# The probabilities of two attentions are scaled by 1/sum on ScalarE instead of VectorE

## The chip, the core and the metric

The kernel runs on one core of a Trainium2 chip. The metric is the device time of one launch in microseconds (us). Before the change three runs took 2502.02 to 2503.47 us, with a median of 2502.81.

The engines are named as the profile names them: PE is TensorE's matmuls, PEld its weight loads, DVE is VectorE, ACT is ScalarE, POOL is GpSimd, SP is SyncE. Each works through its own queue of instructions in order and waits on semaphores for the others.

## The reference

The program is a hybrid layer (convolution beside an attention over the 256 best keys, or fewer, then a mixture of 64 experts) followed by two more layers: one with latent attention (MLA) and a SwiGLU, one with differential attention and a SwiGLU. 512 tokens, 1024 channels, 8 heads in each attention, all in f32. The change touches the softmax of the first two attentions. In the first layer (`dsa_attention`) it is

```python
s = jnp.einsum('bqhd,bqkhd->bhqk', qb, ks).astype(jnp.float32) * (Dh ** -0.5)
s = jnp.where(valid[:, None], s, -jnp.inf)
p = jax.nn.softmax(s, axis=-1).astype(vs.dtype)
o = jnp.einsum('bhqk,bqkhd->bqhd', p, vs)
```

and in the latent attention (`_mla_mixer`)

```python
logits = jnp.where(_chunk_mask(i * Q_BLOCK, s), logits * scale, NEG_BIG)
p = jax.nn.softmax(logits, axis=-1)
o = jnp.einsum('bhqk,bkhd->bqhd', p.astype(v.dtype), v, preferred_element_type=jnp.float32)
```

## The kernel before, in words

Every f32 product that must keep its precision is made from three matmuls (`mm3`, L228 to L230) of operands split into a high and a low part. `split` (L220, L221) makes these: ACT copies the high part, then DVE subtracts it from the source to get the low part. Names ending in h and l, such as `pth` and `ptl`, `qth` and `qtl`, `wh` and `wl`, are such pairs.

The first layer's and the latent attention share `attend`. Its items are the pairs (head h, query tile qt), 8 heads by 4 tiles of 128 queries, 32 in each attention. Tile qt sees `nk` = (qt + 1) * 128 keys, so four tiles of a head are 128, 256, 384 and 512 columns wide. Each item goes through five stages, and `pipeline` runs, in step s, stage A of item s, B of item s - 1, C of item s - 2, F of item s - 4 and E of item s - 3, in this order:

- A: logits, matmuls into a PSUM bank (L228 to L230, and L818 or L1859 for the mask).
- B: `soft_exp`. DVE takes the row maximum, negated (`nm`, L923), ACT the exponential with `nm` as its bias and the row sum as a second output (`p` and `sum`, L926; the read of the accumulator is an instruction of its own).
- C: DVE takes `rsum`, the reciprocal of `sum` (L943), and multiplies `p` by it in place (L945).
- E: `place` transposes `p` by matmuls with the identity, a 128x128 block each (L233), and splits the result: ACT `pth` (L220), DVE `ptl` (L221).
- F: for the last tile of a head alone, the value product from `pth` and `ptl`, and the split of its result (`qth`/`qtl` in the first layer, `mixoh`/`mixol` in the latent attention).

After the stages of a step `pipeline` takes units from a generator of other work ("filler" below), on average 1.2 a step in the first layer (the rest of the convolution, then half of the output projection, L792 to L799, L847, L848) and 0.8 in the latent attention (the projections of the next pairs of heads, `qd`, `kd`, `vd`, then half of the output projection, L1687). The filler fetches weights, each with a wide split on ACT and DVE (`wh`, `wl`, 128x1536 to 128x2048). Everything is issued in the order in which the Python code runs, so the order on each engine is that of the steps. The tiles `p` rotate through three buffers, `sum` through six. The differential attention has a softmax of its own, with a multiply at another line (L2047), and does not use `attend`.

Of the kernel before, what the change touches and what calls it, by code (L numbers as in the profile page):

```python
# [15 lines left out]
AF = mybir.ActivationFunctionType  # L16
OP = mybir.AluOpType
# [163 lines left out]
class _K:  # L181
# [747 lines left out]
    def attend(self, heads, logits, value, fill=None, n=0, bufs=3, ready=None):  # L929

        V = self.nc.vector
        lg, pr, pT = {}, {}, {}

        def A(h, qt):
            lg[h, qt] = logits(h, qt)

        def B(h, qt):
            pr[h, qt] = self.soft_exp(lg.pop((h, qt)), (qt + 1) * 128, "p", bufs)

        def C(h, qt):  # L940
            p, sm = pr[h, qt]
            rs = self.sm([128, 1], "rsum", bufs=4)
            V.reciprocal(rs, sm)  # L943
            nk = (qt + 1) * 128
            V.tensor_scalar(p[:, :nk], p[:, :nk], rs, None, OP.mult)  # L945

        def E(h, qt):
            if qt == 0:
                pT[h] = [self.slot(F32R, x).rearrange("p (a b) -> p a b", b=512) for x in ("pth", "ptl")]
            self.place(pT[h], qt, pr.pop((h, qt))[0])  # L950

        def F(h, qt):
            if qt == NT - 1:
                value(h, pT.pop(h))
        self.pipeline([(h, qt) for h in heads for qt in range(NT)], [(A, 0), (B, 1), (C, 2), (F, 4), (E, 3)], fill, n, ready)
# [1200 lines left out]
```

## Time and profile before

| | us |
|---|---|
| median of three runs | 2502.81 |
| the profiled execution | 2503.96 |
| its span, first to last instruction | 2502.2 |
| PE busy | 2321.1 (93%) |
| DVE busy | 1449.6 (58%) |
| ACT busy | 941.1 (38%) |
| L945, 64 instructions on DVE | 24.8 |

The profiled execution is one launch under the hardware profiler, and all rows are of it. Busy time is summed over the span and says nothing on the place. The chain of waits is followed back from the last instruction: at each piece either the instruction before it on its engine, or the one that released it. A row of the view of waits tells how long an engine sat idle in front of a line and what ended that; where the profile could not tell a semaphore's releaser it says "issue". A row of a timeline gives start, duration, engine, line, operation and tiles, and in brackets the idle time before it. PEclk is the granted clock of TensorE as a share of its higher level, 2.4 GHz; 0.50 is the lower one, 1.2 GHz. L945 runs from 265.0 to 1399.4 us, in two stretches of 32 instructions.

### The profile page before, as it was taken

How to read it: one execution, taken by the hardware profiler on the slowest of the kernel's cores; microseconds unless marked ns; L12 is line 12 of the kernel's file. 1: busy time of each engine (PE TensorE's matmuls, PEld its weight loads, DVE VectorE, ACT ScalarE, POOL GpSimd, SP SyncE). 2: the span in 40 equal slices, each digit the busy share in tenths (PEclk: the TensorE clock that was granted, in tenths of full speed). 3: DMA queues.
4: the chain of work that ended last, by engine and by line, in shares of the span. 5: the costliest groups of instructions: out<-in, count | busy, mean ns of one | idle time of the engine just before them, and what ended most of it. 6: DMA issues, size and time to landing. Idle time of an engine off the chain costs nothing.

```text
span 2502.2 us, 29499 instructions
## 1 busy us (share of the span) xinstructions
PE 2321.1 (93%) x11088; PEld 1805.0 (72%) x11088; DVE 1449.6 (58%) x2454; ACT 941.1 (38%) x1382; POOL 281.6 (11%) x184
## 2 busy tenths in 40 slices
PE   8877998799989999999699999999999998999998
PEld 4655767567667776676577788888888876888886
DVE  4599666666666765665576653333655657433235
ACT  1552443345545555555244222222234432322121
POOL 0652000122322222231000000000000000000000
PEclk9888999899999999999899999999999998999999
DMA  9442134599998999999402332232231121323310
GB/s 335 169 143 68 51 114 169 175 318 339 331 321 284 378 352 335 369 375 332 125 18 83 103 118 73 96 118 76 83 119 51 51 102 55 114 84 116 102 69 34
DMA packets 195009, 422.15 MB, mean 169 GB/s; under 512 B 21329, under 2 KB 99921, under 8 KB 186545
## 3 DMA queue, kind: packets, MB, share of 16 engines
q1 hardware_dynamic: 169984, 353.44, 39.8%
q0 software_dynamic: 12944, 39.20, 6.7%
q10 hardware_dynamic: 11938, 27.62, 3.0%
q8 instruction: 88, 1.44, 0.2%
q14 instruction: 55, 0.45, 0.1%
HBM read 390.78 MB, written 35.52 MB: 170 GB/s over the span
## 4 chain that ended last, share of the span: by engine, by line
PE 68%; DVE 16%; DMA 9%; ACT 4%; issue 2%; POOL 1%; ACTq 0%; SPq 0%; DVEq 0%; POOLq 0%
PE b L228 20%; PE b L229 19%; PE b L230 19%; PE b L1412 6%; DMA wraw<-in_w_dram 5%; DVE wl L221 4%; PE b L233 4%; DMA acc<-eo,isc 3%; ACT wh L220 2%; DVE work L754 1%; PE b L547 1%; DVE m L750 1%; DMA wraw<-in_w_ada_dram 1%; PE b L2029 1%; DVE y L1651 1%
## 5 line engine op out<-in xcount | busy, mean ns | idle before, releaser
L221 DVE TENSOR_TENSOR wl<-wraw,wh 128x2048 fp32r<-128x2048 f32 (+2 forms) x247 | 557.4, 2260 | 515.5 <-ACT wh L220 465.4
L220 ACT ACTIVATE wh<-wraw 128x2048 fp32r<-128x2048 f32 (+2 forms) x247 | 463.3, 1880 | 152.6 <-DVE wl L221 64.6
L228 PE MATMUL b<-xtl,wh 128*128 128x512 f32 (+1 forms) x928 | 343.5, 370 | 2.9 <-DVE xtl L221 2.9
L229 PE MATMUL b<-xth,wl 128*128 128x512 f32 (+1 forms) x928 | 341.6, 368 | 0.0
L230 PE MATMUL b<-xth,wh 128*128 128x512 f32 (+1 forms) x928 | 341.5, 368 | 0.0
L228 PE MATMUL b<-wl,xet 128*128 128x512 f32 x536 | 231.4, 432 | 15.3 <-DVE wl L221 14.9
L1412 PE MATMUL b<-wraw,aet 128*128 128x512 f32 x536 | 242.0, 595 | 0.8 <-ACT aet L1404 0.8
L230 PE MATMUL b<-wh,xet 128*128 128x512 f32 x536 | 214.2, 400 | 0.0
L229 PE MATMUL b<-wh,xet 128*128 128x512 f32 x536 | 213.1, 398 | 1.1 <-DVE xet L221 0.9
L228 PEld LDWEIGHTS b<-xtl,wh 128*128 128x128 f32 x928 | 176.1, 190 | 32.7 <-DVE xtl L221 3.6
L230 PEld LDWEIGHTS b<-xth,wh 128*128 128x128 f32 x928 | 175.8, 189 | 28.7
L229 PEld LDWEIGHTS b<-xth,wl 128*128 128x128 f32 x928 | 176.0, 190 | 28.0
L1412 PEld LDWEIGHTS b<-wraw,aet 128*128 128x128 f32 x536 | 98.9, 191 | 101.6 <-issue 97.0
L1217 POOL DMA_INDIRECT acc<-eo,isc x67 | 111.4, 1662 | 517.4 <-DMA acc<-eo,isc 126.9
L228 PE MATMUL b<-wl,ath 128*128 128x512 f32 x352 | 137.1, 390 | 0.0
L230 PE MATMUL b<-wh,ath 128*128 128x512 f32 x352 | 136.9, 389 | 0.0
L229 PE MATMUL b<-wh,atl 128*128 128x512 f32 x352 | 136.9, 389 | 0.0
L228 PEld LDWEIGHTS b<-wl,xet 128*128 128x128 f32 x536 | 103.2, 193 | 42.5 <-issue 20.3
L926 ACT ACTIVATE p<-b,nm 128x128 f32<-128x128 f32 (+3 forms) x128 | 67.0, 526 | 166.8 <-DVE nm L923 128.0
L229 PEld LDWEIGHTS b<-wh,xet 128*128 128x128 f32 x536 | 102.8, 192 | 28.6 <-issue 6.5
L230 PEld LDWEIGHTS b<-wh,xet 128*128 128x128 f32 x536 | 102.6, 191 | 23.1
L1933 ACT ACTIVATE t2k<-b 128x512 f32<-128x512 f32 x44 | 26.3, 599 | 185.9 <-PE b L230 185.9
(456 smaller groups left out, 4115.8 us busy)
## 6 DMA issues: line engine op xcount, KB each, us to landing
wraw<-in_w_dram SPq DMA_DIRECT2D x256, 512.0 KB, 11.2
wraw<-in_w_dram SPq DMA_DIRECT2D x64, 1024.0 KB, 9.7
wraw<-in_ffn_w_gu_dram SPq DMA_DIRECT2D x44, 1024.0 KB, 5.1
wraw<-in_w_ada_dram SPq DMA_DIRECT2D x24, 1024.0 KB, 10.4
wraw<-in_ffn_w_down_dram SPq DMA_DIRECT2D x20, 1024.0 KB, 4.9
wraw<-in_diff_w_in_dram SPq DMA_DIRECT2D x12, 1024.0 KB, 5.2
wraw<-in_w_in_dram SPq DMA_DIRECT2D x8, 1024.0 KB, 8.0
wraw<-in_w_in_dram SPq DMA_DIRECT2D x12, 512.0 KB, 5.0
```

The lines of the kernel that those rows point to most:

```text
L220: nc.scalar.activation(H, x, AF.Copy)
L221: nc.vector.tensor_tensor(out=L, in0=x, in1=H.bitcast(F32), op=OP.subtract)
L228: mm(ps, s[0], m[1], start=start, stop=False)
L229: mm(ps, s[1], m[0], start=False, stop=False)
L230: mm(ps, s[0], m[0], start=False, stop=stop)
L233: self.nc.tensor.transpose(ps, x, self.ident[:x.shape[0], :x.shape[0]])
L547: nc.tensor.matmul(ps, cb[:, kc, :], w[:, kk, :], start=False, stop=kc == 7)
L750: V.max(m8[qt - 1], work(qt))
L926: nc.scalar.activation(p[:, :nk], ps[:, :nk], AF.Exp, bias=nm, accum_out=sm)
L1217: nc.gpsimd.indirect_dma_start(out=acc, out_offset=IndirectOffsetOnAxis(ap=idx, axis=0), in_=o, in_offset=None, compute_op=OP.add)
L1412: nc.tensor.matmul(ps, aT[:, f * 128:f * 128 + 128], w[:, f, c], start=f == 0, stop=f == 1)
L1933: nc.scalar.activation(sg, pss[j], AF.Silu)
```

## The change

One line of `attend`'s stage C:

```diff
             rs = self.sm([128, 1], "rsum", bufs=4)
             V.reciprocal(rs, sm)
             nk = (qt + 1) * 128
-            V.tensor_scalar(p[:, :nk], p[:, :nk], rs, None, OP.mult)
+            self.nc.scalar.activation(p[:, :nk], p[:, :nk], AF.Copy, scale=rs)
```

The reciprocal stays on DVE. The multiply becomes an activation of the function Copy with a per-row scale, in place. PE, POOL and SP keep their instructions and their order; the matmuls that transpose `p` wait for ACT where they waited for DVE.

On ACT, in the first layer (the steps around 355 to 362 us; `p` are the probabilities, `rsum` the reciprocal of their sum, `pth` the high part of the transposed ones). Before:

```order
L926 ACTIVATE p,sum<-b,nm 128x512 [waits DVE_49]
L220 ACTIVATE pth<-b 128x2x128 [waits PE_49]
L926 ACTIVATE p,sum<-b,nm 128x128 [waits DVE_49]
L220 ACTIVATE pth<-b 128x3x128 [waits PE_49]
L926 ACTIVATE p,sum<-b,nm 128x256 [waits DVE_49]
L220 ACTIVATE pth<-b 128x4x128 [waits PE_49]
```

and now:

```order
L926 ACTIVATE p,sum<-b,nm 128x512 [waits DVE_49,Activation_49]
L945 ACTIVATE p<-p,rsum 128x384 [waits DVE_49,Activation_49]
L220 ACTIVATE pth<-b 128x2x128 [waits PE_49]
L926 ACTIVATE p,sum<-b,nm 128x128 [waits DVE_49,Activation_49]
L945 ACTIVATE p<-p,rsum 128x512 [waits DVE_49,Activation_49]
L220 ACTIVATE pth<-b 128x3x128 [waits PE_49]
L926 ACTIVATE p,sum<-b,nm 128x256 [waits DVE_49,Activation_49]
L945 ACTIVATE p<-p,rsum 128x128 [waits DVE_49,Activation_49]
L220 ACTIVATE pth<-b 128x4x128 [waits PE_49]
```

Between the exponential of one item and the copy `pth` of the item two before it now stands the scale of the item between them.

On DVE, in the latent attention, behind a weight split (around 1339 to 1346 us; `wl` is the low part of the weights, `qd` and `kd` are the next heads' queries and keys). Before:

```order
L221 TENSOR_TENSOR wl<-wraw,wh 128x2048
L224 SCALAR_TENSOR_TENSOR qd<-b,qd 128x512
L923 TENSOR_REDUCE nm<-b 128x1
L943 RECIPROCAL rsum<-sum 128x1
L945 TENSOR_SCALAR p<-p,rsum 128x384
L221 TENSOR_TENSOR ptl<-b,pth 128x2x128
L221 TENSOR_TENSOR kd<-b,kd 128x512
```

and now:

```order
L221 TENSOR_TENSOR wl<-wraw,wh 128x2048
L224 SCALAR_TENSOR_TENSOR qd<-b,qd 128x512
L923 TENSOR_REDUCE nm<-b 128x1
L943 RECIPROCAL rsum<-sum 128x1
L221 TENSOR_TENSOR ptl<-b,pth 128x2x128
L221 TENSOR_TENSOR kd<-b,kd 128x512
```

Here `ptl` follows `rsum` at once, and the transposes of the 384-wide `p` no longer wait for DVE.

## Rows read from the trace of the kernel before

**Rows 1.** The page, part 1: busy us, share of the span and instructions.

```profile
PE 2321.1 (93%) x11088; PEld 1805.0 (72%) x11088; DVE 1449.6 (58%) x2454; ACT 941.1 (38%) x1382; POOL 281.6 (11%) x184
```

**Rows 2.** Windows: stretch, us, busy us by engine (PE, PEld, DVE, ACT, POOL), PEclk, DMA, GB/s.

```profile
264.00:376.00 112.00, 104.52 (x519) 76.86 (x518) 74.83 (x166) 46.83 (x113) 0.00 (x0) 1.00 0.26 83
1292.00:1400.00 108.00, 104.33 (x570) 85.39 (x568) 67.18 (x165) 50.01 (x127) 0.00 (x0) 0.97 0.19 69
```

**Rows 3.** Waits, first layer's attention, 262 to 400: us in total, times, longest.

```profile
DVE ptl L221 <- ACT pth L220: 19.2, 23, 2.3
...
ACT pth L220 <- PE b L233: 6.4, 7, 1.7
...
PE b L233 <- DVE p L945: 4.0, 4, 1.3
```

**Rows 4.** Waits, latent attention, 1287 to 1405 us.

```profile
DVE ptl L221 <- ACT pth L220: 13.7, 23, 1.1
...
ACT mixoh L220 <- PE b L230: 10.0, 7, 4.1
...
PE b L233 <- DVE p L945: 3.6, 4, 2.5
```

**Rows 5.** Groups by line (L945), line L657, groups by form from 262 to 400.

```profile
L945 DVE TENSOR_SCALAR p<-p,rsum 128x128 f32<-128x128 f32 (+1 forms) x64 | 24.8, 387 | 2.3
...
L657 ACT ACTIVATE adap<-wraw,cs x64: 706/713/774, 67.3 to 208.9; 128x512 f32<-128x512 f32 x64
...
L945 DVE TENSOR_SCALAR p<-p,rsum 128x512 f32<-128x512 f32 x8 | 3.9, 487 | 0.3
...
L926 ACT ACTIVATE p<-b,nm 128x128 f32<-128x128 f32 x8 | 2.9, 368 | 19.3 <-DVE nm L923 11.6 <-DVE rsum L943 7.7
```

**Rows 6.** Chain of waits, first layer: start us, us, what (first, middle, last of eleven).

```profile
298.19 0.10 ACT p L926
...
358.28 0.78 ACT p L926 x2
359.06 0.28 ACT pth L220
...
372.98 0.78 ACT p L926 x2
```

**Rows 7.** Chain of waits through L945, first and last of six.

```profile
277.72 0.50 DVE p L945
...
1371.34 0.43 DVE p L945
```

**Rows 8.** Timeline, 1342 to 1344 us.

```profile
1342.77 0.69 ACT L926 ACTIVATE p<-b,nm 128x512 f32<-128x512 f32 x1 [3.02 <-DVE nm L923]
1342.85 0.42 DVE L945 TENSOR_SCALAR p<-p,rsum 128x384 f32<-128x384 f32 x1
1343.32 0.31 PEld L233 LDWEIGHTS b<-ident,p 128*128 128x128 f32 x3 [0.87 <-DVE p L945]
...
1343.36 0.19 ACT L926 ACTIVATION_READ_ACCUMULATOR p<-b,nm 128x1 f32 x1
1343.45 0.37 ACT L220 ACTIVATE pth<-b 128x256 fp32r<-128x256 f32 x1
```

**Rows 9.** Timeline, exponential and next transposes, the first and last of six places.

```profile
298.19 0.58 ACT L926 ACTIVATE p<-b,nm 128x384 f32<-128x384 f32 x1 [3.86 <-DVE rsum L943]
...
298.96 0.20 PEld L233 LDWEIGHTS b<-ident,p 128*128 128x128 f32 x2
...
1397.22 0.69 ACT L926 ACTIVATE p<-b,nm 128x512 f32<-128x512 f32 x1 [1.39 <-DVE nm L923]
...
1397.77 0.48 PEld L233 LDWEIGHTS b<-ident,p 128*128 128x128 f32 x3
```

**Rows 10.** Windows of TensorE alone, latent attention: stretch, us, PE busy, PEclk, DMA, GB/s.

```profile
1369.00:1372.00 3.00, 0.52 (x4) 1.00 1.04 414
1372.00:1381.00 9.00, 9.00 (x30) 0.62 0.51 195
```

## The prediction

> **What bounds the kernel now.** Over the whole span TensorE is busy 93%, VectorE (DVE) 58%, ScalarE (ACT) 38% [rows 1], but an average says nothing on a change that touches two short stretches, so I read those: the first layer's attention from 264 to 376 us and the latent attention from 1292 to 1400 us [rows 2]. In both the granted clock is at or near full speed (1.00 and 0.97), TensorE is busy 104.5 of 112 and 104.3 of 108 us, DVE 75 and 67, ACT 47 and 50. So ACT has the more room, and TensorE is idle only 7.5 and 3.7 us. Which engine sets the pace is then a matter of order, not of load.
>
> Next I read who waits for whom in the two stretches. In the first, DVE waits 19.2 us in 23 pieces for ACT's `pth` before it can subtract `ptl`, while ACT's `pth` itself waits only 6.4 us for TensorE's transposes [rows 3]. In the latent attention DVE waits 13.7 us for `pth`, again 23 times [rows 4]. TensorE's own waits for the scaled probabilities are 4.0 and 3.6 us, four times each [rows 3, 4]. This is one loop, once a step: DVE row maximum `nm`, ACT exponential, ACT `pth`, DVE `ptl`, DVE filler work, next `nm`. DVE's multiply L945 stands beside ACT's exponential, not in that loop.
>
> Last, the chain of waits. In the first layer, from 298 us to 373 us, it goes eleven times through ACT's exponential of a step and, directly behind it, an ACT copy (`pth` or `qth`); the first and last of these, and one whole passage at 358 us, are in [rows 6]. Six times the chain goes instead through DVE's L945, usually into the transposes: at 277.72, 301.20 and 374.59 us and in the latent attention at 1315.37, 1342.85 and 1371.34 us [rows 7]. The rest of the two stretches is mostly TensorE on the chain.
>
> **What is removed.** 64 multiplies on DVE, 24.8 us [rows 5]. I value this at nothing: in 46 of the 64 steps DVE would only wait longer for `pth` right behind it [rows 3, 4], and no step gets its probabilities earlier, because the scale still needs `rsum`, which stands on DVE behind the same `nm` and the same filler work. What covers it is the wait for `pth`; were that gone, the 18 other steps at 24.8/64 = 0.39 us would be a gain of 7.0 us, which I keep for a rival.
>
> **What is added.** 64 ACT copies with a per-row scale, SBUF to SBUF. The trace has this form at one width: L657, 128x512, median 713 ns [rows 5]. For the other widths I take the slope of the exponential, 0.69 us at 512 columns [rows 8] and 0.37 at 128 [rows 5], so 0.107 us for 128 more: 0.39, 0.50, 0.61 and 0.71 us, 2.21 us a head and 35.4 us for the 16 heads. Bounds for a 512-wide one: 0.49 us, if ACT took what DVE takes (487 ns [rows 5]), and 0.77, the longest of L657. I take 0.71, since it is the same instruction. Neighbours on ACT overlap: at 1342.77 us the accumulator is read 0.10 us before the exponential ends, and `pth` starts 0.10 us before that read ends, at 1343.45 [rows 8]. So `pth` starts where the exponential ends, and the scale put between them moves `pth` by its length less 0.10 us: 0.45 us on the mean, 29 us over 64 steps, if nothing hid any of it.
>
> The Trainium skill, "Perfetto Trace Analysis", section "Optimizing Scalar/DVE Operations", says that an operation either engine can do is faster on DVE where a DVE performance mode exists, and that handing it to Scalar may make sense if DVE is saturated; the first half agrees with 487 against 713 ns, and the second is not met, as DVE is busy 67% and 62% here [rows 2, 5]. Read as engine time, the rule would give 35.4 - 24.8 = 10.6 us slower, if all of it counted.
>
> **What of it lies on the path.** What counts by the rows is the place in ACT's queue: exponential of one step, then the scale of the step before, then `pth`. Behind a late scale stand the transposes on TensorE; behind a late `pth` stand `ptl` and the next `nm`, and on ACT the high halves of the filler's splits.
>
> (a) The eleven passages of the chain through exponential and copy. Each gets the scale between the two; by the widths met (three of 128, three of 256, three of 384, two of 512) this is 3 x 0.39 + 3 x 0.50 + 3 x 0.61 + 2 x 0.71 = 5.9 us, less 11 x 0.10 = **4.8 us**.
>
> (b) The six passages through L945. At 1342.85 the multiply ends at 1343.27 and the transposes load at 1343.32 [rows 8]. On ACT the scale can start only where `pth` started, 1343.45, and ends 0.61 later at 1344.06: 0.79 us late. Four of the six have this shape (about 0.8 each, 3.2), the one at 277.72 has a short exponential and a wide scale (0.5), and the one at 374.59 has no exponential beside it (0.2): **4.0 us**.
>
> (c) Places next in line. TensorE's transposes of a step come a whole step after its scale, and in about 45 of the 64 the probabilities lie ready for more than 0.9 us; there the later scale is covered by the logits matmuls and filler matmuls in between. At six places off the chain they lie ready for less than the scale is late. First: exponential at 298.19 for 0.58, so scale to 299.27, transposes at 298.96, short by 0.31. Last: 1397.22 + 0.69 + 0.61 = 1398.52 against 1397.77, short by 0.75 [rows 9]. With 0.27, 0.45, 0.69 and 0.37 at 1302.64, 1328.58, 1356.03 and 1374.32, worked out alike from their rows: **2.8 us**. Some are absorbed by a stall ahead of them; against that, lags of 0.45 us a step can add up over three or four steps before they reach TensorE. I let the two cancel.
>
> (d) The clock. At 1369 to 1372 us TensorE is idle for all but 0.5 of 3 us behind a weight split, and over the next 9 us the granted clock is 0.62 on the mean, so part of them at the lower level [rows 10]: 9 x 0.38 = 3.4 us lost. Stalls of the same make stand in the first layer at 278, 349 and 373 us, without a fall (clock 1.00 over the whole stretch [rows 2]); each grows by 0.5 to 0.9 us. I count one new fall, at 3.4 us; bounds none and three (10 us).
>
> No added wait touches SP's or POOL's queue, and the weight loads wait only on splits that are late with the rest. What follows each attention needs its last head, so I see nothing that gives the delay back. Sum: 4.8 + 4.0 + 2.8 + 3.4 = **15.0 us slower**. The profiled execution took 2503.96 us (span 2502.2), 1.15 above the median of the three runs, 2502.81: 2503.96 + 15.0 = 2519.0 for such an execution, **2518 us** as a median.
>
> **The rivals.** About 0.2%, 5 us, is what a measurement of this kernel can tell from no change.
>
> *Hidden.* TensorE is busy 93 and 97% of the stretches, and most steps have over 0.9 us in hand; ACT waits 10.0 us for the value product before `mixoh` [rows 4], room that a later ACT could use up. If the chain's eleven passages had a neighbour path with as much slack, only part of (b) would be left: 0 to 5 us, 2503 to 2508. Against it: the chain of waits is in itself a lower bound, and (a) and (b) lengthen its own pieces by 8.8 us.
>
> *The loop takes over.* Every step grows by 0.45 us and TensorE waits in each: 29 us, 2503.96 + 29 - 1.15 = 2532; with less hidden before and more falls of the clock the same end is reached. For it: nine of the eleven passages lie within 32 us, from 341 to 373 us, nearly one in every step. Against it: ACT waits for TensorE at 6.4 us (`pth`, first layer) and 10.0 us (`mixoh`) [rows 3, 4], which the lag would first fill. It decides where these waits are used up in the first steps of a head.
>
> *Faster.* DVE is the busier of the two, and its queue holds the filler and the weight splits. If in the 18 steps where `ptl` did not wait for `pth` it still does not, DVE is 7.0 us ahead, and 2496 us follows. For it: ACT idles over half of each stretch. Against it: in these steps DVE mostly waited for another ACT copy one instruction before. It decides if those ACT copies do not move, which needs the scale to fit in front of them while ACT waits for TensorE.
>
> **How the numbers follow.** Forecast, 6 to 20 us slower: 0.63. Loop takes over, 20 to 31: 0.17. Hidden: 0.13. Faster: 0.07. The first two are slower by over 0.2%: 0.80; hidden is the same, 0.13; 0.07 faster. The range leaves out the faster rival, the lower half of the hidden one and what lies past the loop's 29 us: 2506 to 2533.
>
> **What would show it.** Right: 64 ACT instructions at L945 of 0.39 to 0.71 us; DVE's wait for `pth` grows by some 10 us or more in each attention; TensorE's transposes wait for ACT's L945 more than the 4.0 and 3.6 us that they wait for DVE's; both stretches end later, the first by some 7 us (10 with a fall of the clock) and the latent by some 5, and the rest moves along unchanged. Wrong: if the two stretches keep their length with `pth` late, the slack was larger than read; if they shorten, DVE's queue was the bound; if the stretches grow by less than the total, the difference was lost in a later stage.

## The result, and the profile after

The changed kernel took 2524.3 us (median of six runs), the kernel before 2503.1 in the same runs: a ratio of 1.0088, 95% interval 1.0069 to 1.0107, so some 22 us slower (17 to 27). The forecast was 15 slower, the range reached to 2533. Direction and range were right. The size was short by a third: 15 lies below the interval, and 22 lies past the forecast's own 6 to 20 us, in the band of the rival *The loop takes over*. The runs below show that the waits were sized not far off in sum, and the loss by the clock much too small.

The profiled execution of the changed kernel has a span of 2529.2 us, 27.0 more than before; it is the second slowest of the six. Its page, part 1, answers to [rows 1]:

```profile
PE 2327.6 (92%) x11088; PEld 1810.5 (72%) x11088; DVE 1424.3 (56%) x2390; ACT 969.4 (38%) x1446; POOL 280.6 (11%) x184
```

DVE lost 25.3 us of work, ACT gained 28.3 (less than the some 35 us of 64 scales, as neighbours on ACT overlap), TensorE has the same 11088 matmuls. The two attentions, in the columns of [rows 2]:

```profile
264.00:380.00 116.00, 104.77 (x505) 76.33 (x504) 61.12 (x129) 57.97 (x138) 0.00 (x0) 0.99 0.26 80
...
1310.00:1430.00 120.00, 105.39 (x570) 85.70 (x570) 56.42 (x131) 64.14 (x157) 0.00 (x0) 0.96 0.20 71
```

TensorE is idle 11.2 us in the first and 14.6 in the second, against 7.5 and 3.7. These windows do not hold quite the same matmuls (505 records in the first, 519 before). Cut at the same instructions, as below, TensorE's idle time goes from 8.8 to 14.8 us in the first attention and from 13.4 to 21.8 in the latent one, 14.4 us more in all. The line L945 itself and who waited for it:

```profile
L945 ACT ACTIVATE p<-p,rsum x64: 388/551/726, 265.6 to 1424.7; 128x128 f32<-128x128 f32 x16, 128x256 f32<-128x256 f32 x16, 128x384 f32<-128x384 f32 x16, 128x512 f32<-128x512 f32 x16
...
  PEld b L233: 22.2, 16
  PE b L233: 17.7, 14
```

The prices are as forecast (0.39 to 0.73 us, against 0.39 to 0.71). TensorE waits 17.7 us for it, where it had waited 7.6 for DVE's. The waits, first layer (262 to 400 us), which answer to [rows 3]:

```profile
DVE ptl L221 <- ACT pth L220: 37.2, 24, 2.7
...
PE b L233 <- ACT p L945: 7.9, 6, 2.9
...
ACT pth L220 <- PE b L233: 1.8, 2, 1.3
```

and latent attention (1310 to 1430 us), which answer to [rows 4]:

```profile
DVE ptl L221 <- ACT pth L220: 35.6, 24, 1.6
...
PE b L233 <- ACT p L945: 9.7, 8, 4.4
...
ACT mixoh L220 <- PE b L230: 5.9, 7, 3.4
```

DVE's wait for `pth` has grown by 18 and 22 us, more than the 12 us of multiplies that each stretch lost. ACT's own waits for TensorE have shrunk, from 6.4 to 1.8 (`pth`) and from 10.0 to 5.9 (`mixoh`): that is slack, and part of it is being used up. In the chain of waits of the changed kernel L945 now stands in the loop, here two steps of the first layer:

```profile
314.89 0.60 DVE nm L923
...
316.17 0.19 ACT p L926
316.37 0.51 ACT p L945
316.87 0.28 ACT pth L220
317.15 0.02 issue
317.18 0.42 DVE ptl L221
317.60 0.20 DVE nm L923
...
318.16 0.19 ACT p L926
318.35 0.61 ACT p L945
318.97 0.38 ACT pth L220
```

Maximum, exponential, scale, `pth`, `ptl`, next maximum, with no TensorE between. The chain passes L945 22 times in the first layer and 16 times in the latent attention, 38 of 64, where eleven exponentials and six multiplies were counted before.

**Where the 27 us lie.** I cut each profiled execution at the same instructions: start of the first exponential of `attend`; of the first square of the residual rows after the attention (L865); of the first and the last expert's silu (L1395); of the latent attention's first mask matmul (L1859); of the first silu of the next block (L1933); and the end. The stretch ahead of the first cut, 261.8 to 265.8 us long, is left out.

| us | first attention | to the experts | experts | to the latent | latent attention | rest | span |
|---|---|---|---|---|---|---|---|
| before | 130.0 | 85.8 | 703.4 | 102.8 | 179.3 | 1036.6 | 2502.2 |
| the change | 138.3 | 87.3 | 707.9 | 103.9 | 189.7 | 1037.4 | 2529.2 |
| first only | 141.1 | 84.5 | 698.8 | 103.8 | 178.3 | 1035.9 | 2506.8 |
| latent only | 130.0 | 85.8 | 704.1 | 102.4 | 190.8 | 1035.7 | 2512.7 |
| ahead (e9) | 132.0 | 87.0 | 701.9 | 103.9 | 182.5 | 1036.1 | 2509.2 |
| early (e4) | 135.5 | 86.9 | 703.9 | 102.8 | 203.1 | 1036.6 | 2530.7 |
| apart (e10) | 131.3 | 88.2 | 706.9 | 102.9 | 178.2 | 1035.9 | 2505.2 |
| none (e6) | 130.0 | 85.8 | 702.7 | 104.9 | 178.0 | 1036.4 | 2500.5 |
| dummy (e7) | 130.0 | 85.8 | 707.1 | 102.7 | 187.8 | 1037.3 | 2514.7 |
| twice (e8) | 152.5 | 86.9 | 704.3 | 102.5 | 201.1 | 1035.8 | 2544.9 |
| narrow (e11) | 134.1 | 87.6 | 704.5 | 104.1 | 181.3 | 1036.6 | 2510.3 |
| wide (e12) | 137.0 | 85.7 | 704.0 | 102.5 | 187.6 | 1036.0 | 2516.8 |

The first attention is 8.3 us longer and the latent 10.4. The experts' stretch, 4.5 longer here, differs by as much between executions without the change: 702.7 to 707.1 us in the four kernels that leave the scale off ACT in the first attention (before, latent only, none, dummy), 704.3 on the mean, and 698.8 to 707.9 in the eight that put it there, 704.0 on the mean. So nothing is read from it.

The same program is not equally long each time either. The change and first only run the same program up to the end of the first attention, but take 138.3 and 141.1 us there. TensorE alone, the change and then first only, in the columns of [rows 10]:

```profile
264.70:403.00 138.30, 123.50 (x594) 0.99 0.26 82
...
264.40:405.50 141.10, 127.36 (x594) 0.95 0.25 81
```

Idle for 14.8 and 13.7 us, TensorE was busy 3.9 us longer with the same matmuls in the second, at a lower mean granted clock (0.95 against 0.99). Differences of 1 to 3 us between rows of the table can come from that alone.

### The profile page after: what moved, and what is told of

It reads as the page before. It is cut to its first block, busy times and chain, and to the rows that moved or that the text cites. A ratio compares the mean times of both kernels' runs of the same rounds, so it can differ in the third digit from the quotient of the medians.

```text
span 2529.2 us, 29563 instructions
## 1 busy us (share of the span) xinstructions
PE 2327.6 (92%) x11088; PEld 1810.5 (72%) x11088; DVE 1424.3 (56%) x2390; ACT 969.4 (38%) x1446; POOL 280.6 (11%) x184
## 4 chain that ended last, share of the span: by engine, by line
PE 70%; DVE 16%; ACT 5%; DMA 5%; issue 2%; POOL 1%; ACTq 0%; DVEq 0%; POOLq 0%; SPq 0%
PE b L228 20%; PE b L229 19%; PE b L230 19%; PE b L1412 7%; PE b L233 4%; DVE wl L221 3%; DMA acc<-eo,isc 3%; ACT wh L220 2%; DVE work L754 1%; PE b L547 1%; DVE m L750 1%; DMA wraw<-in_w_ada_dram 1%; ACT p L945 1%; DVE ptl L221 1%; DVE nm L923 1%
## 5 line engine op out<-in xcount | busy, mean ns | idle before, releaser
L1933 ACT ACTIVATE t2k<-b 128x512 f32<-128x512 f32 x44 | 26.3, 598 | 185.9 <-PE b L230 185.9
## 6 DMA issues: line engine op xcount, KB each, us to landing
wraw<-in_w_dram SPq DMA_DIRECT2D x256, 512.0 KB, 11.2
```

The lines of the kernel that those rows point to most:

```text
L1933: nc.scalar.activation(sg, pss[j], AF.Silu)
```

## The experiments

Theory A: the loss is the scale's place in ACT's queue, between two instructions of ACT that DVE waits for in turn, and the late probabilities. Theory B: it is ACT's extra 35 us of work, wherever it stands. Theory C: part of it arises among the experts.

**One attention at a time.** Diff against the change (e1; e2 has the condition reversed):

```diff
-            self.nc.scalar.activation(p[:, :nk], p[:, :nk], AF.Copy, scale=rs)
+            if ready is None:
+                self.nc.scalar.activation(p[:, :nk], p[:, :nk], AF.Copy, scale=rs)
+            else:
+                V.tensor_scalar(p[:, :nk], p[:, :nk], rs, None, OP.mult)
```

> The scale is on ACT in the first layer's attention alone. Theory A, place in ACT's queue (the scale between the exponential and the transposed copy lengthens the loop of DVE and ACT, and the probabilities come late): about 9 us slower than the kernel before, all of it between 264 and 400 us, where the profile after shows the stage that follows beginning 8.7 us later. Theory C, part of the loss arises in the mixture of experts, whose stretch was some 5 us longer in the profile after: 14 us. Theory B, the time follows ACT's extra 17.7 us of work: up to 17 us.

> The scale is on ACT in the latent attention alone. Theory A: about 10 us slower, all of it between 1286 and 1425 us, with one stall of over 4 us behind the weight split at the end; with e1 it adds to the whole change's 21 us (9 + 10, the rest noise). Theory C: 10 us here, and 14 in e1. If the sum of the two is well below 21 us, the two stretches act on each other.

First only: 1.0050 (1.0038 to 1.0063), 9.5 to 15.8 us. Latent only: 1.0061 (1.0049 to 1.0073), 12.3 to 18.3 us. Each attention is longer where its own multiply moved, and the other is not (table: 141.1 and 190.8). The times do not decide against theory C: its 14 us for the first alone lie in the interval, and A's 9 just below it. The profiles speak against it: the experts are no longer with the scale on ACT in the first attention than without (704.0 and 704.3 us). What the timed runs lose beyond the two attentions is taken up at the end of this section. Together the two come to some 28 us, the whole change to 22; their intervals overlap.

**The scale ahead of the exponential.** Stage C is moved ahead of B:

```diff
-        self.pipeline([...], [(A, 0), (B, 1), (C, 2), (F, 4), (E, 3)], fill, n, ready)
+        self.pipeline([...], [(A, 0), (C, 2), (B, 1), (F, 4), (E, 3)], fill, n, ready)
```

> As the change, but reciprocal and scale of an item are issued ahead of the next item's maximum and exponential in each step; the number and kind of instructions stay. Theory A: the scale then runs on ACT while DVE takes the maximum, the loop grows by the reciprocal alone (0.15 us a step, 5 us an attention at most) and behind a weight split the probabilities are ready some 0.3 us earlier than before: between 5 us faster and 5 us slower than the kernel before. Theory B: 21 us slower, as the change.

1.0043 (1.0029 to 1.0056), 7 to 14 us slower, half of the change's loss and more than I expected from A. The same 64 instructions cost 2.0 and 3.2 us in the two stretches instead of 8.3 and 10.4; the rest of the timed loss lies outside them. My arithmetic left out that the exponential behind the scale starts late where a 512-wide scale meets a 128-wide maximum: in its profile, at 349.76 us, the scale takes 0.72 us, the maximum is there at 349.85, and the exponential starts at 350.38. Theory B falls all the same: with the work unchanged the time is not.

**A step early.** Stage C follows E in the exponential's own step:

```diff
-        ... [(A, 0), (B, 1), (C, 2), (F, 4), (E, 3)], fill, n, ready)
+        ... [(A, 0), (B, 1), (F, 4), (E, 3), (C, 1)], fill, n, ready)
```

> As the change, but reciprocal and scale of an item follow in the same step as its exponential, behind the transposed copy and its low part and ahead of the filler, a step earlier. Theory A: the scale runs on ACT beside the filler's work on DVE, no copy stands behind it, and the probabilities are ready a step early, so TensorE's waits for them (4.0 and 3.6 us before) go: 3 to 10 us faster than the kernel before. Theory B: 21 us slower, as the change.

1.0119 (1.0103 to 1.0134), 30 us slower, worse than the change: the plainest miss. TensorE's waits for the probabilities did go down against the change (to 2.4 and 3.7 us, from 7.9 and 9.7), in the latent attention only to what they were before (3.6), and the latent stretch is 203.1 us. There TensorE waits 15.6 us for `ptl` (1.7 before), and it is busy some 10 us longer with the same matmuls, at a lower granted clock (0.91 over the stretch, 0.96 before). Its timeline:

```profile
1345.32 0.56 DVE L221 TENSOR_TENSOR ptl<-b,pth 128x384 fp32r<-128x384 f32 x1 [0.91 <-ACT pth L220]
1345.80 0.15 DVE L943 RECIPROCAL rsum<-sum 128x1 f32<-128x1 f32 x1
1346.05 0.40 ACT L945 ACTIVATE p<-p,rsum 128x128 f32<-128x128 f32 x1 [0.75 <-DVE rsum L943]
1346.35 0.37 ACT L220 ACTIVATE vd<-b 128x256 fp32r<-128x256 f32 x1
1346.75 0.42 DVE L221 TENSOR_TENSOR vd<-b,vd 128x256 fp32r<-128x256 f32 x1 [0.80 <-ACT vd L220]
1347.09 0.41 DVE L923 TENSOR_REDUCE nm<-b 128x1 f32<-128x256 f32 x1
```

I had taken the filler for DVE's work alone. In the latent attention it is splits, high half on ACT, low half on DVE: ACT now waits for `rsum` behind `ptl`, the high half `vd` waits behind the scale, DVE waits for `vd`, and the next maximum stands behind that. DVE waits 9.5 us for `vd` in 10 pieces, where it waited 0.6 in 2 before. The scale is in the loop again, and ACT's split too. The rule left to be tried is narrower: a scale costs no wait on ACT only where no instruction behind it is one DVE is waiting for.

**Reciprocal early, scale ahead of the exponential.** So the two halves of C are parted: the reciprocal behind `ptl`, the scale at the opening of the next step.

```diff
+            pr[h, qt] = p, rs
+
+        def C2(h, qt):
+            p, rs = pr[h, qt]
             nk = (qt + 1) * 128
             self.nc.scalar.activation(p[:, :nk], p[:, :nk], AF.Copy, scale=rs)
...
-        ... [(A, 0), (B, 1), (C, 2), (F, 4), (E, 3)], fill, n, ready)
+        ... [(A, 0), (C2, 2), (B, 1), (F, 4), (E, 3), (C, 1)], fill, n, ready)
```

> The scale on ACT where ACT idles: the reciprocal of an item follows at the end of its own step, behind the low part of the transposed copy and ahead of the filler, and the scale opens the next step's work on ACT, ahead of the exponential that waits for DVE's maximum. Same instructions as the change. Theory A (place in ACT's queue; a scale costs what it puts between an ACT and a DVE instruction that wait for each other): no copy or split stands behind the scale that DVE waits for, the loop grows by the reciprocal alone, 0.11 us a step, and TensorE's waits for the probabilities go: both stretches within 3 us of the kernel before, 5 us faster to 4 us slower in all. Theory B (ACT's extra 35 us of work): 21 us slower, as the change.

The stretches come out as expected, +1.3 and -1.1 us, and in the first layer TensorE waits 1.5 us, once, for the scale, where it waits 7.9 in the change. The whole did not: 1.0034 (1.0019 to 1.0049), 5 to 12 us slower, against at most 4. In its profile 2.4 us lie between the attention and the experts, where TensorE's idle time is as before (20.6 us) and its busy time 2.5 us longer, and 3.5 among the experts, where executions differ by as much without the change. The timed runs show a lower clock over the whole span: their mean granted clock is 0.9615, against 0.9639 of the kernel before in the same runs.

**No multiply at all** leaves the probabilities unscaled:

```diff
-            V.tensor_scalar(p[:, :nk], p[:, :nk], rs, None, OP.mult)
```

> Leaves the multiply out on both engines, so the probabilities stay unscaled; the reciprocals stay. What DVE's multiply was worth where it stood. The document's reading: next to nothing in the loop (the wait for the transposed copy takes its place), and the six places where TensorE waited for it gain up to 0.4 us each: 0 to 4 us faster than the kernel before. The rival (DVE's queue was the bound): 7 us faster or more.

0.9997 (0.9985 to 1.0009), between 3.8 us faster and 2.3 slower: nothing. The first stretch is 130.0 us as before, the latent 1.3 shorter. DVE spends the freed time waiting for `pth`, 28.9 us in the first layer against 19.2 [rows 3]:

```profile
DVE ptl L221 <- ACT pth L220: 28.9, 23, 2.7
```

So at most some 4 us were to be won by taking this multiply out of DVE's queue, and no version that was run is measurably faster than the kernel before.

**ACT's queue without the late probabilities.** The kernel before, and in the latent attention an ACT copy on a tile `dm` that nobody uses, at the place of the change's scale:

```diff
             V.tensor_scalar(p[:, :nk], p[:, :nk], rs, None, OP.mult)
+            if ready is not None:
+                self.nc.scalar.activation(self.dm[:, :nk], self.dm[:, :nk], AF.Copy, scale=rs)
```

> The kernel before, with DVE's multiply, and in the latent attention alone an ACT copy of the same width and with the same per-row scale on a tile that nobody uses, at the place where the change puts its scale: ACT's queue of the change, but probabilities on time. To be held against the latent-only change, 10.5 us in its stretch. If that loss is the late transposed copy and the longer loop: 7 to 10 us. If it is the late probabilities alone (terms (b) and (c) of the prediction): 0 to 3 us.

The latent stretch is 187.8 us, 8.5 longer, of the 11.5 of latent only and the 10.4 of the change (all runs: 1.0039, 1.0026 to 1.0053, 6 to 13 us). The probabilities are on time; what comes late is `pth`, and with it `ptl` and the value product on TensorE (latent attention, 1287 to 1420 us):

```profile
DVE ptl L221 <- ACT pth L220: 24.0, 24, 1.1
...
PE b L228 <- DVE ptl L221: 7.7, 5, 3.3
...
PE b L233 <- DVE p L948: 4.9, 6, 2.5
```

Before, TensorE waited 1.7 us for `ptl` here, and 3.6 for `p`. TensorE's idle time grows by 5.9 us, of 9.2 in latent only and 8.4 in the change. So two thirds to four fifths of the loss in this stretch are the longer loop. The other 2 to 3 us are put down to the late probabilities by difference alone, and two executions of one program differ by as much.

**Twice.**

```diff
             self.nc.scalar.activation(p[:, :nk], p[:, :nk], AF.Copy, scale=rs)
+            self.nc.scalar.activation(p[:, :nk], p[:, :nk], AF.Copy, scale=1.0)
```

> The change with a second ACT copy of the same width in place behind the scale. If the slack of the steps is used up by the first scale, every further us on ACT between exponential and transposed copy counts: 64 x 0.45 = 29 us on top of the change, some 50 us over the kernel before. If the loss is a fixed number of places (17 on or next to the chain), as the prediction counted: some 15 us on top, 36 in all.

1.0178 (1.0163 to 1.0194), 45 us. The second copy adds 14.2 us to the first stretch of the change and 11.4 to the latent, 25.6 of the 29 it would cost with nothing hidden, where the first scale added 18.7. But 8.8 of the 25.6 are TensorE busy longer with the same matmuls, at a lower granted clock. Its idle time grows by 16.8 us, after 14.4 for the first scale. And held against the stretches of the one-attention kernels (141.1 and 190.8), the first scale adds 22.6 and the second 21.7; the timed runs say 22.0 and 22.5. So about half of the 29 us shows as idle time each time, and that the first scale uses up the slack is not shown.

**By width.** `if qt < 2` in e11, `if qt >= 2` in e12 choose ACT, else DVE multiplies.

> The scale on ACT for the 128- and 256-wide tiles of each head alone, DVE keeps the 384- and 512-wide ones. If the loop of DVE and ACT sets the pace, the loss goes with the time put between exponential and transposed copy: (0.39 + 0.50 - 0.20) of (2.21 - 0.40) us a head, 38% of the change's some 22 us: 8 us. If it goes by the places that the prediction counted (late probabilities stand almost all at wide tiles; narrow scales on the chain are 3 x 0.39 + 3 x 0.50 - 0.60 = 2.1 us): 2 to 3 us.

> The scale on ACT for the 384- and 512-wide tiles alone. By the loop: 62% of some 22 us, 14 us. By the places that the prediction counted: nearly the whole loss, 18 to 20 us.

Narrow: 1.0019 (1.0008 to 1.0029), 2 to 7 us; wide: 1.0059 (1.0043 to 1.0074), 11 to 19. In the stretches 4.1 + 2.0 = 6.1 and 7.0 + 8.3 = 15.3, in TensorE's idle time 2.5 and 9.8 us. Narrow by its time holds the places' 2 to 3 us and not the loop's 8, wide holds the loop's 14 and the places' 18. Wide scales count for more than their 62% of the time put into the loop (80% of the idle time), so neither reading is right as it stands, and this test does not choose between them.

**What the time is made of.** Two numbers together come near every measured time, within 2.4 us but for early (4.2). One is TensorE's idle time in the two attentions, from the profiled execution, less that of the kernel before (22.2 us); it is of one execution each, and the same first attention gave 5.9 and 4.9 in two. The other is the clock: of each timed run, the span times what its mean granted clock lacks to 1, less the same for the kernel before in the same runs (for the change, in the 47 later ones; 89.9 us, clock 0.9640). It is known to 2 to 4 us, and is an upper bound, since a low clock costs nothing while TensorE is idle.

| us, more than before | idle, attentions | clock | sum | time |
|---|---|---|---|---|
| the change | 14.4 | 9.8 | 24.2 | 22.0 |
| first only | 4.6 | 7.2 | 11.8 | 12.5 |
| latent only | 9.1 | 5.6 | 14.7 | 15.3 |
| ahead | 4.1 | 7.1 | 11.3 | 10.8 |
| early | 16.2 | 17.8 | 34.0 | 29.8 |
| apart | 0.6 | 6.4 | 7.0 | 8.5 |
| none | -1.6 | 2.5 | 0.9 | -0.8 |
| dummy | 5.9 | 4.4 | 10.3 | 9.8 |
| twice | 31.2 | 15.7 | 46.9 | 44.5 |
| narrow | 2.5 | 2.5 | 5.0 | 4.8 |
| wide | 9.8 | 5.4 | 15.2 | 14.8 |

So theory A accounts for the idle part, and the place decides it: 0.6 us (apart) to 16.2 (early) for the same 64 scales. The other part is TensorE at its lower clock level for longer, much of it outside the two attentions. Why apart, with hardly more idle time, loses 6.4 us there, no run shows.

## Why the prediction was right, and where it was short

*What is removed is worth nothing*: right, shown by the kernel without a multiply. With that the rival "faster" falls: there were no 7.0 us to be had (at most some 4), and DVE's waits took up what it was given.

*The price of one scale*: right, 0.39 to 0.73 us, median 0.55. The Trainium skill ("Perfetto Trace Analysis", section "Optimizing Scalar/DVE Operations") makes handing work to Scalar a question of whether DVE is saturated; the prediction read that as engine time, 10.6 us. The same work cost from some 8 us (apart) to 30 us (early), depending on where it stood, so engine time does not decide here.

*(a), the chain's passages through the exponential, 4.8 us*: the mechanism was right, and the size in the first attention too: with (b) and (c) the terms there come to 6.6 us, and TensorE's idle time grew by 5.9 (4.9 in first only). But (a) was counted on the chain of before, which in the latent attention does not pass through the exponential, so the step gave 0 there; the dummy copy measured 5.9 us of idle time. So a loop that runs beside the chain had little slack. In the changed kernel the chain runs through 38 scales.

*(b) and (c), late probabilities, 2.4 + 2.5 us in the latent attention*: by the dummy run 2 to 3 us, so probably too large. (The items of (b) add up to 3.9, not 4.0, and nothing hangs on it.) For the first layer they weren't parted from (a).

*"I let the two cancel"* in (c), lags that add up against stalls that absorb them: it held for the first attention and failed for the latent one, where all terms of waiting come to 4.9 us and TensorE's idle time grew by 8.4. In sum the waits were 14.4 us against 11.6.

*(d), one new fall of the clock, 3.4 us*: this is the term that was mis-sized most. TensorE alone, the changed kernel, in the first attention and behind the latent one's weight split:

```profile
356.00:359.00 3.00, 1.39 (x7) 1.00 1.03 411
359.00:362.00 3.00, 3.00 (x14) 0.56 1.17 313
362.00:365.00 3.00, 3.00 (x15) 0.87 0.47 114
...
1391.00:1394.00 3.00, 0.57 (x4) 0.94 1.05 412
1394.00:1397.00 3.00, 1.04 (x5) 0.50 1.03 401
1397.00:1400.00 3.00, 3.00 (x12) 0.50 0.54 208
1400.00:1403.00 3.00, 3.00 (x9) 0.50 0.00 0
1403.00:1406.00 3.00, 3.00 (x12) 0.86 0.00 0
```

After TensorE has been idle half of 356 to 359 us the granted clock drops, in part to the lower level, for about two stretches: 3 x 0.44 + 3 x 0.13 = 1.7 us lost. The fall in the latent attention [rows 10] stayed behind the same weight split but lasted longer, 5.1 us lost against 3.4. Together that is the 3.4 us of the forecast, by luck: in first only the first attention alone lost some 7 us (141.1 x 0.05). Over the whole span the timed runs lost up to 9.8 us to the clock, give or take 4. The prediction looked for falls in the two attentions alone.

So the forecast fell 7 us short, by up to 6 us of the clock and some 3 of waits in the latent attention, and the range held because it reached to the next rival. *The loop takes over* (29 us) was as near as the forecast: 22 lies halfway between them, though TensorE's idle time, 14.4 us, is far from its 29.

## What to carry to other kernels

Where two engines hand work to each other in a loop, ask of an added instruction what stands behind it in its queue that the other engine is waiting for; the load of the engines (42% and 46% busy on ACT here) does not answer that. A removed instruction that stood beside a wait gives nothing. The chain of waits before a change is a fair count of what an added delay costs where the chain passes through the loop (6.6 us against 5.9 in the first attention), but it misses a loop that runs beside it with little slack (none counted against 5.9 in the latent one). Of the sum over all steps, 29 us, about half came to be idle time of TensorE. And count the clock by itself, over the whole program and over many runs: here it was up to 10 of 22 us, and one profile does not show it.

## What was not expected of the hardware

In the latent attention the four transfers that ACT issues for the reload (L1678) stand in ACT's queue ahead of a weight split. The changed kernel's chain of waits shows one of them alone at 1.73 us:

```profile
1386.99 1.73 ACTq L1678
1388.76 0.45 ACTq L1678
1389.23 0.47 ACTq L1678
```

and by the timelines the four held ACT for 3.08 us there and 1.86 before. That is not the change's doing: they held it for 2.90 us in first only, whose latent attention is that of before, and for 3.44 in the kernel without a multiply. TensorE's longest wait for the scaled probabilities in the changed kernel's attentions, 4.4 us, lies behind it, so part of its growth from 2.5 is not the scale's; in first only that wait is 3.5. Why an issue is sometimes slow, no run shows.
